# Splitting the weights once and reloading both parts from DRAM, in a hybrid decoder layer on one core

## The chip, the core and the metric

The kernel runs on one core of a Trainium2 chip. Times are microseconds (us) of device time, from one execution of the whole program. The median of three runs of the kernel before is 2899.07 us (2898.01 to 2899.21). A change of about 0.2%, 5.8 us, is the least that a measurement of this kernel can tell from no change.

The engines are called as the profile calls them: PE is the matrix engine and PEld its loading of weights, DVE the vector engine, ACT the scalar engine, POOL the general engine, and SP the engine that only issues transfers. Each works through its own instructions in a fixed order.

## What is computed

The reference is one decoder layer over 2048 tokens of width 1024, batch 1, all in 32-bit floats. Cut to what matters here:

```python
mod = (cs @ ada_w[l] + ada_b[l])[:, None, :]
sh1, sc1, g1, sh2, sc2, g2 = jnp.split(mod, 6, axis=-1)
h = rmsnorm(x, norm1_g[l]) * (1.0 + sc1) + sh1
p = h @ w_in[l]
...
y = jnp.concatenate([ya, yb, yc], axis=-1) * mix_beta[l]
x = x + g1 * (y @ w_out[l])
h = rmsnorm(x, norm2_g[l]) * (1.0 + sc2) + sh2
x = x + g2 * swiglu(h, ffn_w_gate[l], ffn_w_up[l], ffn_w_down[l])
```

ya, yb and yc come from three recurrent mixers (RG-LRU, HGRN2, RWKV-7) that read columns of p. Five weight matrices multiply activations of every token: w_in (1024 x 3456), w_out (1024 x 1024), w_gate and w_up (1024 x 2816 each) and w_down (2816 x 1024).

## The kernel before

**Tiling.** Activations lie transposed, 128 features by 512 tokens in a tile. The 2048 tokens make four blocks, b = 0 to 3. Weights lie in DRAM in chunks of 128 output columns: w_in has 27 of them (128 x 1024 each), w_out 8, w_gate and w_up 22 each, and w_down 8 chunks of 2816.

**Precise products from reduced floats.** A 32-bit product is made from three matmuls of the faster format (R in the code): every operand is split into a high part, which is the value rounded to that format, and a low part, which is the rest. `project` (line 238) adds high x high, high x low and low x high for each 128 rows of the contraction: three matmuls of 128x128 by 128x512 on line 248. The product of 512 contraction rows, one piece of weights, is twelve matmuls.

**Weights.** `load_w` (line 227) cuts the weights that it is given into pieces of 512 contraction rows. For each it loads the raw piece on SP's queue into a tile `wr` (`raw_w`, line 129; three buffers, 256 KB), and then splits it (`split_v`, line 219): ACT copies it to `wh` with rounding (recorded on line 78), and DVE subtracts to get `wl` (line 221). `wh` and `wl` have four buffers each. A buffer of `wr` comes free with its subtraction, one of `wh` and `wl` with the last matmul that reads it. The conditioning weights (`ada_w`, line 172 through line 140) use `wr` too after the start.

**How often.** A piece is loaded and split anew each time that a block needs it. The stage of w_in takes the blocks in pairs (0 and 1, then 2 and 3): of the 27 chunks, 18 serve both blocks of a pair from one load, and the first four and last five of the order are loaded once for each block. That makes 36 chunks in a pair, 72 in all, two pieces each. After it, for each block in turn, `w_out_products` (line 892) goes through the 8 chunks of w_out, and `ffn` (line 922) through 22 of w_gate and w_up (`ffn_up`, line 906) and through w_down in six groups of four (the last of two) feature tiles for each of eight output chunks, so that its last eight pieces have 256 rows only.

**Mixers.** The products of w_in go to DRAM (`pd`, stored on SP's queue, line 867). The mixers of a block load their columns on ACT's queue (line 461), run as long chains of small instructions on PE, DVE and ACT with round trips through DRAM (the tiles NL, NX and GIQ, lines 583 to 611), and store their results in `yd`. `load_y` (line 883) loads these for `w_out`; POOL does the subtraction there (line 217).

**What sets the order.** A planner orders each engine's instructions when the program is built, from its own estimates of times. An instruction is taken when its inputs and a buffer for its output are there in the plan, the lowest number first; the numbers come from the levels of line 62: "out" before "load" before "feed" before "mix" before "dense". Loads and splits of weights are "load", loads of x and stores of `pd` are "feed", the mixers are "mix", the matmuls of line 248 are "dense", and so are the stores of the output (line 943). On the chip each engine keeps the planned order whatever the true times are. `w_after` (lines 131 to 134) holds a load of weights behind another load at the start.

**Norms.** After w_out and before the next w_in there is a norm: squares are summed, `rstd_of` (line 288) splits the sum into tiles of `w_parts` (line 224) and sends it through PE with ones (lines 296 to 299), and `make_h` (line 322) makes the split activations `hh` and `hl` for the next products.

Of the kernel before, what the change touches and what calls it, by code (L numbers as in the profile page):

```python
# [10 lines left out]
F = mybir.dt.float32  # L11
R = mybir.dt.float32r
# [8 lines left out]
TB = 512  # L21
# [30 lines left out]
def hybrid_kernel(ctx, tc, x, par, ada_w, w_in, rgw, igw, w_up, a_up, g_up, w_out,  # L52
# [169 lines left out]
        return i  # L222

    def w_parts():
        return dp.tile([128, TB], R, name="wh", bufs=4), dp.tile([128, TB], R, name="wl", bufs=4)

    def load_w(src, fn):
        ws = []
        with level("load"):
            for c in range(0, src.shape[1], TB):  # L230
                n = min(TB, src.shape[1] - c)
                w = raw_w(src[:, c:c + n])
                hi, lo = w_parts()
                fn(w[:, :n], hi[:, :n], lo[:, :n])
                ws.append((hi, lo))
        return ws

    def project(h, *cols):
# [113 lines left out]
    with level("feed"):  # L352
        xsum = None
        xt = [load_x(x, 0, k) for k in range(KC)]
        w_after[:] = last_load
        tiles = {}
        for k in range(KC):
            for part, tile in ((1, tr_), (0, th_)):
                tiles[part, 0, k] = ada_tile(tile(), part, 0, k)
        for k in range(KC):  # L360
            for part, tag in ((1, "hh"), (0, "hl")):
                tiles[part, 1, k] = ada_tile(dp.tile([128, TB], F, name=tag, bufs=16), part, 1, k)
        for k in range(KC):
            xsum = square_sum(xsum, xt[k], k)
        rs = rstd_of(xsum)

        def shift_and_scale(half, pe):
            drain(zip_longest(*(ada(part, half, lambda k, part=part: tiles[part, half, k], pm_, xs_, pe)
                                for part in (1, 0))))

        shift_and_scale(0, (0, 2, 4))
        head = IN_ORDER[:2]
        W = {c: load_w(w_in[c], split_v) for c in head}
        w_after[:] = last_load
        h0 = make_h(lambda k: xt[k], rs, A1, B1, ks=range(4))
        ahead = x_stats([1], 8, tr_, th_, lambda: (tile_of("th", R)[:, 0:TB], tile_of("th", R)[:, 0:TB]))
        next(ahead)
        shift_and_scale(1, (0, 1))
        h0 += make_h(lambda k: xt[k], rs, A1, B1, ks=range(4, KC))
# [6 lines left out]
    with level("mix"):  # L386
# [14 lines left out]
        w = th_()  # L401
# [450 lines left out]
    def w_in_products(h, cols, side):  # L852

        n = 0
        while n < len(cols):

            cs_ = cols[n:n + 2] if n == 0 and len(h) == 1 else cols[n:n + 1]
            ws = [W.pop(c) if c in W else load_w(w_in[c], split_v) for c in cs_]
            for i, b in enumerate(h):
                for j, (c, p) in enumerate(zip(cs_, project(h[b], *ws))):  # L860
                    with level("feed"):
                        t = xs_()
                        if (n + i + j) % 2:
                            act(t, p)
                        else:
                            V.tensor_copy(t, p)
                        SP.dma_start(pd[c, :, b * TB:(b + 1) * TB], t)
                    next(side, None)
            n += len(cs_)
# [22 lines left out]
    def w_out_products(b, ys, before):  # L892
        x1, s = [], None
        for d in range(KC):
            ws = load_w(w_out[d], split_v)
            t = load_x(x, b, d)
            p, = project(ys, ws)
            with level("out"):
                stt(t, p, G1[:, d:d + 1], t, OP.mult, OP.add)
            if d == 0:  # L900
                before()
            s = square_sum(s, t, d)
            x1.append(t)
        return x1, rstd_of(s)

    def ffn_up(h, f):
        if f:
            p, = project(h, load_w(w_gate[f], split_v))
        else:
            p, pu = project(h, load_w(w_gate[f], split_v), load_w(w_upf[f], split_v))  # L910
        t = xs_()
        with level("out"):
            act(t, p, AF.Silu)
        if f:
            pu, = project(h, load_w(w_upf[f], split_v))
        with level("out"):
            V.tensor_mul(t, pu, t)  # L917
        g = parts_()
        split_v(t, *g)
        return g  # L920

    def ffn(b, x1, rs):
        h = make_h(lambda k: x1[k], rs, A2, B2, "silu_and_others", over=False)
        gs, s, ys = [], None, None
        for f0 in range(0, NF, 4):
            n = min(4, NF - f0)
            while len(gs) < min(f0 + n + (2 if f0 + n + 2 >= NF else 1), NF):
                gs.append(ffn_up(h, len(gs)))
            if len(gs) == NF and ys is None and b + 1 < NB:
                ys = load_y(b + 1)  # L930
            for d in range(KC):
                p, = project(gs[f0:f0 + n], load_w(w_down[d][:, f0 * 128:(f0 + n) * 128], split_v))
                with level("out"):
                    stt(x1[d], p, G2[:, d:d + 1], x1[d], OP.mult, OP.add)
                if f0 + n == NF:
                    s = square_sum(s, x1[d], d, n=1 if b + 1 < NB else 2)
# [96 lines left out]
```

## Time and profile before

| | before |
|---|---|
| median of 3 runs | 2899.07 us |
| profiled execution, its own time | 2902.32 us |
| span from first to last instruction in it | 2900.5 us |
| mean granted PE clock | 0.979 |
| HBM read, written | 286.53 MB, 48.23 MB |

The profiled execution is 3.25 us over the median, and 1.8 us of its time lie outside the span. The profile counts an engine as busy from the start of its first to the end of its last overlapping instruction; matmuls overlap, so their busy times don't add up. "Idle before" is the time that an engine stood still before an instruction, and the name behind the arrow is what ended the wait. A name with a small q is the engine's own queue, where transfers are issued. The granted clock is the share of its full speed at which PE was let run.

### The profile page before, as it was taken

The page shows a single profiled execution, that of the slowest core. Times are in us where ns is not written, and L with a number is a line of the kernel's source. Part 1 is how long each engine was busy: PE and PEld are TensorE (multiplying, and loading weights), DVE is VectorE, ACT ScalarE, POOL GpSimd, SP SyncE. Part 2 cuts the span into 40 slices and gives each one's busy share as a digit, 9 for nine tenths or more (in the row PEclk, how much of TensorE's full clock was granted, in tenths as well). Part 3 has the DMA queues.
Part 4 walks back from the last instruction along what each step waited for, and adds up shares of the span by engine and source line. Part 5 has one row for each costly group of instructions (what it writes and reads, how often), then busy time and mean ns, then how long its engine had stood idle before and what let it go on. Part 6 is the DMA issues. An engine that isn't in the chain of part 4 may idle for free. (4 is left out here: it accounts for less than half of the span.)

```text
span 2900.5 us, 41766 instructions
## 1 busy us (share of the span) xinstructions
PE 2771.4 (96%) x14842; PEld 2197.8 (76%) x14842; DVE 1985.5 (68%) x4617; ACT 1506.6 (52%) x2521; POOL 82.4 (3%) x67
## 2 busy tenths in 40 slices
PE   7999998999998899999999999999899999999998
PEld 6777776777776677777767777777677788788886
DVE  7765867777577687777887877778776444644345
ACT  4528456254645846567576465675563433533333
POOL 2000000000001000000100000010000001000000
PEclk9999999999999999999999999999999999999999
DMA  7534445434344233333442323335233233433332
GB/s 253 155 116 131 135 145 185 141 119 131 99 128 138 84 95 87 106 103 95 142 138 84 113 70 116 98 103 162 65 93 101 88 98 116 145 99 98 98 95 87
DMA packets 235041, 337.52 MB, mean 116 GB/s; under 512 B 73041, under 2 KB 78673, under 8 KB 234833
## 3 DMA queue, kind: packets, MB, share of 16 engines
q1 hardware_dynamic: 160144, 285.55, 31.7%
q10 hardware_dynamic: 74688, 49.31, 6.9%
q8 instruction: 117, 1.92, 0.3%
q14 instruction: 92, 0.75, 0.1%
HBM read 286.53 MB, written 48.23 MB: 115 GB/s over the span
## 5 line engine op out<-in xcount | busy, mean ns | idle before, releaser
L248 PE MATMUL pd<-hh,wh 128*128 128x512 f32 x3232 | 1290.5, 400 | 31.5 <-ACT hh L78 31.1
L248 PE MATMUL pd<-hl,wh 128*128 128x512 f32 x3232 | 1290.6, 399 | 4.9 <-DVE hl L81 2.7
L248 PE MATMUL pd<-hh,wl 128*128 128x512 f32 x3232 | 1290.8, 399 | 0.0
L78 ACT ACTIVATE wh<-wr 128x512 fp32r<-128x512 f32 (+1 forms) x752 | 462.1, 619 | 870.0 <-PE pd L248 666.5
L248 PEld LDWEIGHTS pd<-hh,wh 128*128 128x128 f32 x3232 | 613.9, 190 | 161.2 <-ACT hh L78 35.8
L221 DVE TENSOR_TENSOR wl<-wr,wh 128x512 fp32r<-128x512 f32 (+1 forms) x752 | 509.2, 682 | 309.8 <-ACT wh L78 304.4
L248 PEld LDWEIGHTS pd<-hl,wh 128*128 128x128 f32 x3232 | 613.9, 190 | 136.6 <-DVE hl L81 7.8
L248 PEld LDWEIGHTS pd<-hh,wl 128*128 128x128 f32 x3232 | 614.0, 190 | 123.4 <-issue 2.6
L81 DVE SCALAR_TENSOR_TENSOR xs<-pd,Q,xs 128x512 f32<-128x512 f32 x224 | 167.6, 748 | 127.3 <-PE pd L248 120.4
L78 ACT ACT_TABLE_LOAD x190 | 243.8, 1283 | 12.1 <-DMA GIQ<-xd 3.3
L78 ACT ACTIVATE xs<-pd 128x512 f32<-128x512 f32 x140 | 82.8, 591 | 59.7 <-PE pd L248 55.2
L917 DVE TENSOR_TENSOR xs<-pd,xs 128x512 f32<-128x512 f32 x88 | 60.7, 690 | 75.0 <-PE pd L248 73.8
L78 ACT ACTIVATE th<-th 128x512 f32<-128x512 f32 (+2 forms) x153 | 93.5, 612 | 31.1 <-DMA th<-pd 9.0
L78 ACT ACTIVATE hh<-xs 128x512 fp32r<-128x512 f32 x120 | 74.2, 627 | 41.2 <-DVE xs L917 31.3
L78 ACT ACTIVATE hw<-VS,we 64x64 f32<-64x64 f32 x192 | 66.0, 344 | 47.1 <-DVE VS L81 44.0
L599 DVE TENSOR_TENSOR ftmp<-NX,NL 128x30 f32<-128x30 f32 (+4 forms) x360 | 75.2, 209 | 8.8 <-DMA NX<-nd 1.3
L601 DVE TENSOR_TENSOR NX<-NX,ftmp 128x30 f32<-128x30 f32 (+4 forms) x360 | 74.8, 208 | 7.7
L529 POOL MEMSET KG<- 64x1024 f32 x24 | 22.7, 947 | 1775.4 <-PE pm L642 671.0
L78 ACT ACTIVATE xs<-xs 128x512 f32<-128x512 f32 x77 | 47.7, 627 | 41.4 <-DVE xs L81 26.8
L81 DVE SCALAR_TENSOR_TENSOR VS<-pc,we,hw 64x64 f32<-64x64 f32 x168 | 47.4, 282 | 31.7 <-PE pc L653 28.3
L78 ACT ACTIVATE tr<-tr 128x512 f32<-128x512 f32 (+3 forms) x100 | 62.4, 627 | 11.9 <-DVE tr L81 8.3
L221 DVE TENSOR_TENSOR hl<-xs,hh 128x512 fp32r<-128x512 f32 x88 | 61.8, 702 | 5.7 <-ACT hh L78 1.3
(234 smaller groups left out, 2697.6 us busy)
## 6 DMA issues: line engine op xcount, KB each, us to landing
wr<-in_w_gate SPq DMA_DIRECT2D x176, 256.0 KB, 2.6
wr<-in_w_upf SPq DMA_DIRECT2D x176, 256.0 KB, 2.6
wr<-in_w_down SPq DMA_DIRECT2D x160, 256.0 KB, 2.7
wr<-in_w_in SPq DMA_DIRECT2D x144, 256.0 KB, 3.4
pd<-xs SPq DMA_DIRECT2D x108, 256.0 KB, 3.1
xs<-in_x SPq DMA_DIRECT2D x72, 256.0 KB, 4.5
wr<-in_ada_w SPq DMA_DIRECT2D x64, 256.0 KB, 3.4
th<-pd ACTq DMA_DIRECT2D x64, 256.0 KB, 3.5
```

What stands on the lines that cost most here:

```text
L78: return A.activation(o, i, f, **k)
L81: return V.scalar_tensor_tensor(o, a, s, b, op0=op0, op1=op1)
L221: V.tensor_sub(lo, src, hi.bitcast(F))
L248: PE.matmul(p, a[:, c], b, start=(n == 0), stop=(n == tot - 1))
L529: G.memset(KG[o, :, :, e], 0.0)
L599: V.tensor_mul(tv, NX[:, 0:m, j:j + 1].to_broadcast([128, m, n]), NL[:, j:j + 1, j + 1:32].to_broadcast([128, m, n]))
L601: V.tensor_add(NX[:, 0:m, j + 1:32], NX[:, 0:m, j + 1:32], tv)
L917: V.tensor_mul(t, pu, t)
```

## The change

`load_w` gets a name and a number in place of the splitting function, from which a key is made for each piece. At the first use of a key the piece is loaded raw and split as before, into the two halves of one tile `wp` (four buffers, 512 KB each, in place of four of `wh` and four of `wl`), and `wp` is then stored in a new DRAM tile of that key on SP's queue. At any later use of the key both halves are loaded by one transfer on SP's queue straight into `wp`, with no instruction on ACT or DVE. `w_parts`, which the norms use, now takes the halves of a `wp` tile.

```diff
     def w_parts():
-        return dp.tile([128, TB], R, name="wh", bufs=4), dp.tile([128, TB], R, name="wl", bufs=4)
-
-    def load_w(src, fn):
+        t = dp.tile([128, 2, TB], R, name="wp", bufs=4)
+        return t[:, 0], t[:, 1]
+
+
+    parted = {}
+
+    def load_w(src, name, i, first=0):
+
         ws = []
         with level("load"):
             for c in range(0, src.shape[1], TB):
                 n = min(TB, src.shape[1] - c)
-                w = raw_w(src[:, c:c + n])
-                hi, lo = w_parts()
-                fn(w[:, :n], hi[:, :n], lo[:, :n])
-                ws.append((hi, lo))
+                t = dp.tile([128, 2, TB], R, name="wp", bufs=4)
+                key = f"{name}{i}_{first + c}"
+                if key in parted:
+                    k = SP.dma_start(t[:, :, :n].bitcast(F), parted[key])
+                    if w_after:
+                        order(k, w_after.pop())
+                else:
+                    w = raw_w(src[:, c:c + n])
+                    split_v(w[:, :n], t[:, 0, :n], t[:, 1, :n])
+                    parted[key] = tc.dram_tile([128, 2, n], F, name=key)
+                    SP.dma_start(parted[key], t[:, :, :n].bitcast(F))
+                ws.append((t[:, 0], t[:, 1]))
         return ws
...
-        W = {c: load_w(w_in[c], split_v) for c in head}
+        W = {c: load_w(w_in[c], "i", c) for c in head}
...
-            ws = [W.pop(c) if c in W else load_w(w_in[c], split_v) for c in cs_]
+            ws = [W.pop(c) if c in W else load_w(w_in[c], "i", c) for c in cs_]
...
-            ws = load_w(w_out[d], split_v)
+            ws = load_w(w_out[d], "o", d)
...
-            p, = project(h, load_w(w_gate[f], split_v))
+            p, = project(h, load_w(w_gate[f], "g", f))
...
-                p, = project(gs[f0:f0 + n], load_w(w_down[d][:, f0 * 128:(f0 + n) * 128], split_v))
+                p, = project(gs[f0:f0 + n], load_w(w_down[d][:, f0 * 128:(f0 + n) * 128], "d", d, f0 * 128))
```

The other calls in `ffn_up` change in the same way ("g" for w_gate, "u" for w_up).

More of the change, by code (lines that the diff above doesn't have):

```diff
@@ L907, in ffn_up @@
         if f:
-            p, = project(h, load_w(w_gate[f], split_v))
+            p, = project(h, load_w(w_gate[f], "g", f))
         else:
-            p, pu = project(h, load_w(w_gate[f], split_v), load_w(w_upf[f], split_v))
+            p, pu = project(h, load_w(w_gate[f], "g", f), load_w(w_upf[f], "u", f))
         t = xs_()
@@ L914, in ffn_up @@
         if f:
-            pu, = project(h, load_w(w_upf[f], split_v))
+            pu, = project(h, load_w(w_upf[f], "u", f))
         with level("out"):
```

## The prediction

> **What bounds the kernel now.** I read the busy line first, then the groups with shapes kept apart.
>
> ```profile
> PE 2771.4 (96%) x14842; PEld 2197.8 (76%) x14842; DVE 1985.5 (68%) x4617; ACT 1506.6 (52%) x2521; POOL 82.4 (3%) x67
> ```
> ```profile
> L248 PE MATMUL pd<-hh,wl 128*128 128x512 f32 x3232 | 1290.8, 399 | 0.0
> L248 PEld LDWEIGHTS pd<-hh,wh 128*128 128x128 f32 x3232 | 613.9, 190 | 161.2 <-ACT hh L78 35.8 <-issue 4.1 <-ACT wh L78 0.7
> L221 DVE TENSOR_TENSOR wl<-wr,wh 128x512 fp32r<-128x512 f32 x720 | 496.0, 694 | 309.8 <-ACT wh L78 304.4 <-PE pd L248 2.7
> L78 ACT ACTIVATE wh<-wr 128x512 fp32r<-128x512 f32 x720 | 448.9, 629 | 835.1 <-PE pd L248 632.9 <-issue 78.9 <-DMA wr<-in_w_in 50.5
> ```
>
> PE is busy all but 129.1 us of the span. It hardly waits for weights: 0.7 us for `wh`, nothing before a matmul with `wl`. It is the other way round: ACT's splits wait 633 us for PE to free a buffer. Next come PE's rate and idle time by stage (columns: stretch, length, busy us and instructions of PE, PEld, DVE, ACT, POOL; clock, DMA share, GB/s).
>
> ```profile
> 430.00:860.00 430.00, 408.48 (x2405) 322.61 (x2404) 311.14 (x779) 218.86 (x376) 3.79 (x4) 0.98 0.45 135
> 860.00:1440.00 580.00, 556.86 (x3156) 435.52 (x3156) 443.90 (x1090) 352.09 (x586) 28.49 (x22) 0.98 0.36 105
> 1440.00:1960.00 520.00, 500.96 (x2884) 396.01 (x2883) 400.75 (x971) 333.52 (x549) 18.28 (x14) 0.98 0.36 105
> 1960.00:2480.00 520.00, 506.48 (x2493) 402.90 (x2492) 328.29 (x720) 243.29 (x417) 13.32 (x10) 0.98 0.35 104
> 2540.00:2880.00 340.00, 340.00 (x1502) 281.63 (x1501) 141.63 (x213) 103.71 (x172) 0.00 (x0) 1.00 0.32 95
> ```
>
> The last row is the last block, with no mixers beside it: 1502 matmuls in 340 us, 0.226 us each, not one gap. All 9696 matmuls of line 248 at that price are 2195 us; the mixers' PE work fills most of the rest. So the change works on engines that don't bound. It can win only idle time, and the clock lost around it, in the stages that reuse weights: about 430 to 860 (second pair of w_in) and 1440 to 2480 (blocks 1 and 2). Their idle time is 21.5 + 19.0 + 13.5 = 54.0 us. Here are its largest pieces, with two of the last block for comparison.
>
> ```profile
> 493.64 0.79 PE L248 MATMUL pd<-hh,wh 128*128 128x512 f32 x1 [10.66 <-ACT hh L78]
> ```
> ```profile
> 617.88 0.65 PE L653 MATMUL pc<-VS,BK 128*128 128x128 f32 x2 [2.87 <-ACT VS L78]
> ```
> ```profile
> 1956.40 0.79 PE L257 MATMUL pm<-tr,bones 128*128 128x512 f32 x1 [5.76 <-ACT tr L78]
> ```
> ```profile
> 2040.38 0.49 PE L298 MATMUL pd<-wl,aones 128*128 128x512 f32 x1 [1.52 <-DVE wl L221]
> 2042.79 2.08 PE L299 MATMUL pd<-xs,ones 128*128 128x512 f32 x2 [1.91 <-DVE xs L281]
> 2049.12 1.22 PE L248 MATMUL pd<-hh,wh 128*128 128x512 f32 x2 [4.26 <-ACT hh L78]
> ```
> ```profile
> 2517.63 1.12 PE L299 MATMUL pd<-xs,ones 128*128 128x512 f32 x2 [1.57 <-DVE xs L281]
> 2523.02 1.22 PE L248 MATMUL pd<-hh,wh 128*128 128x512 f32 x2 [4.26 <-ACT hh L78]
> ```
>
> A norm costs PE 1.57 + 4.26 = 5.8 us even with nothing beside it. Three norms lie in the reusing stages, so of the 54.0 us at most 54.0 - 17.5 = 36.5 us can go.
>
> **What goes.** First uses are 54 pieces of w_in (27 chunks of two), 16 of w_out, 44 each of w_gate and w_up, 48 of w_down: 206 of 752 splits stay and 546 go, 24 of them of half size, counted here as halves. DVE loses (522 + 12) x 0.694 = 371 us, ACT (522 + 12) x 0.629 = 336 us. Neither is on PE's path as a sum. What counts is which splits stood ahead of a chain that PE waited for:
>
> ```profile
> 1942.53 1.12 DVE L221 TENSOR_TENSOR wl<-wr,wh 128x512 fp32r<-128x512 f32 x1
> ...
> 1947.64 1.10 DVE L221 TENSOR_TENSOR wl<-wr,wh 128x512 fp32r<-128x512 f32 x1
> ```
> ```profile
> 2040.24 1.89 DVE L221 TENSOR_TENSOR wl<-wr,wh 128x512 fp32r<-128x512 f32 x3
> 2042.05 0.69 DVE L281 TENSOR_TENSOR xs<-xs 128x512 f32<-128x512 f32 x1
> ```
>
> - Before the wait of 5.76 us DVE ran without a pause, these two splits among its work: 2.2 us.
> - Three splits stand directly ahead of the sum (line 281) that PE awaits at 2042.79: 1.9 us.
> - The 10.66 us at 493.64 are a norm whose eight loads of x were issued behind a load of weights that waited for a split (SP's timeline below). Its floor is 5.8; I take back the excess, 4.8 us (bounds 0 and 4.8).
> - At 617.88 ACT was late; I take 1.4 of 2.87.
> - The rest is 54.0 - 10.66 - 2.87 - 5.76 - 7.69 = 27 us of smaller waits. DVE loses 371/1985 = 19% of its work; I take 19%, 5 us (bounds 0 and 27 - 5.8 = 21, less the norm of block 1).
>
> ```profile
> 486.50 0.33 SPq L131 DMA_DIRECT2D wr<-in_w_in  x1
> 486.88 4.58 SPq L140 DMA_DIRECT2D xs<-in_x  x8
> ```
>
> Sum 15 us. What also goes is ACT's holding: the 633 us for which it stood before a split until PE freed `wh`, with the mixers' and norms' work behind it in its order. I count that within these waits, because it reaches the time only through them. The clock adds a little:
>
> ```profile
> 480.00:500.00 20.00, 8.73 (x30) 6.26 (x29) 18.57 (x32) 8.22 (x12) 0.00 (x0) 0.66 0.75 246
> 600.00:620.00 20.00, 17.13 (x91) 14.05 (x90) 11.13 (x29) 10.39 (x24) 0.00 (x0) 0.95 0.49 155
> ```
>
> Around a long wait PE runs slow: 0.34 x 20 = 6.8 us of clock are gone in the first of these, and 1 us after the wait of 2.87 in the second. Part of that falls into the wait itself; for waits shortened but mostly not removed I take 3 us (bounds 0 and 10). **Gain: 18 us.** The Trainium skill ("TensorE: Matmul & The Clock Gate", Part 1) has the clock fall only after an idle window of about 3.4 us. By that, shortening the small waits would return no clock; the 0.95 beside a wait of 2.87 us speaks against it as a sharp limit, and the sum would differ by 1 to 3 us.
>
> **What is added.** *Loads twice as long, waiting for PE.* A reload waits on SP for a buffer of `wp`, that is for PE's last matmul on the piece four back, where the raw loads ran up to seven pieces ahead. Behind it on SP stand loads of x and y, for which `make_h`, the residual sums and the splits of y wait on DVE and ACT; stores of `pd` and `out`, whose tiles `xs` the next products' copies out of PE's banks need; and the conditioning loads, for DVE. The plan never puts a load there before its buffer is free in the plan, so the wait costs where the chip falls behind the plan.
>
> ```profile
> wr<-in_w_down SPq DMA_DIRECT2D x160, 256.0 KB, 2.7
> ...
> wr<-in_w_down SPq DMA_DIRECT2D x32, 128.0 KB, 2.0
> ```
>
> 128 KB more cost 0.7 us, so 512 KB should land in 2.7 + 1.4 = 4.1 us (an estimate from these rows). Three pieces lie between: 3 x 12 x 0.226 = 8.1 us of PE's work, more where mixers run or a piece serves two blocks. About 4 us stay spare. In w_down's last eight pieces there are 3 x 6 x 0.226 = 4.1 us against 2.7 and the issue: 1 us spare. I take +3 us for three such ends (bounds 0, and 3 x 8 x 1.36 = 33 if every load there were late by a piece). Traffic in blocks 1 to 3 rises by 176 x 256 KB = 46 MB in some 520 us, from 105 to about 194 GB/s.
>
> *Stores at first use.* 206 stores wait on DVE's split, as the raw load three pieces on already does, so SP loses only their issue:
>
> ```profile
> L867 SPq DMA_DIRECT2D pd<-xs x108: 319/327/424, 61.3 to 879.3; - x108
> ```
>
> A store of `pd` takes 0.327 us to issue, so 206 x 0.327 = 67 us over two stages in which SP mostly waits: nothing. A buffer of `wp` is free only when its store has landed too; four pieces of PE's work lie before its next use, and I count nothing. In block 0 they add 144 x 512 KB over 580 us, 130 GB/s, to 105; the profile has shown
>
> ```profile
> 20.00:40.00 20.00, 18.90 (x84) 17.98 (x83) 14.86 (x27) 5.83 (x8) 0.00 (x0) 1.00 1.03 370
> ```
>
> 370 GB/s, so I put block 0 at nothing; raw loads there still run ahead. But this very window is full, and the first four pieces are stored about there: 2.1 MB at 370 GB/s is 5.7 us on the conditioning loads that the first products need. I take +3 (bounds 0 and 5.7). The norm's use of `wp` in place of `wh` and `wl` takes the same one of four: nothing.
>
> **Sum**: -18 + 3 + 3 = -12 us on the profiled execution: 2902.3 to 2890.3. The median of the runs stood 3.25 us lower: **2887 us**, 0.4% faster.
>
> **Rivals.**
>
> *Nothing moves* (2893 to 2905). The floors stay, freed time on DVE and ACT is filled by mixers that the planner brings forward, and PE meets other waits of the same size. For it: the pure dense row has no gap to win, and the end waits for PE. That reuse fails to happen belongs here too; the keys look distinct, so hardly.
>
> *All contention goes* (2858). 36.5 us of idle and 10 of clock, less the 6 added: 2899 - 41. For it: ACT's long holds on PE vanish from the mixers' path.
>
> *SP becomes the bound* (2928). With PE's own progress at SP's head, a store waiting there holds back the next piece:
>
> ```profile
> SPq L867 <- ACT xs L78: 128.7, 37, 7.8
> SPq L867 <- DVE xs L866: 121.7, 43, 8.5
> ...
> SPq L943 <- DVE xs L81: 29.3, 18, 15.0
> ```
>
> (total, times, longest.) Today seven pieces hide this. It decides from a wait over the 4 us spare: the three longest exceed it by 3.8 + 4.5 + 11 = 19 us, and three new idle stretches lose about 3 us of clock each: +28 with nothing won elsewhere, and the next such waits would add as much again. Against: the mean wait is 1.6 to 3.5 us, and much of it is only SP being early today.
>
> *The mixers' small transfers slow down* (2912). They share the DMA engines with loads of twice the size.
>
> ```profile
> wr<-in_w_gate SPq DMA_DIRECT2D x176, 256.0 KB, 2.6
> ...
> wr<-in_w_in SPq DMA_DIRECT2D x144, 256.0 KB, 3.4
> ```
>
> In the stage of w_in, at 135 GB/s, a load takes 0.8 us more than in the blocks at 105. At 194 I put as much again on four round trips in each of 12 units of RWKV: 38 us, of which a third, as a guess, reaches PE: +13 with nothing won.
>
> ```profile
> 2265.77 209.03 PE pd L248 x922
> ```
>
> Against: the mixers end with 209 us of pure products left in block 2. The Trainium skill ("DMA: Bandwidth & Descriptors", Queues, rings and completion order) says that an engine switches between queues only after a whole packet of several descriptors, which speaks for this rival; no row here shows the switching itself.
>
> **How the numbers follow.** Forecast 0.44 (own range 2866 to 2893), all contention goes 0.11, nothing moves 0.20, SP 0.16, transfers 0.09. Faster by over 0.2% (about what a measurement of this kernel can tell) 0.55, within 0.20, slower 0.25. The range 2857 to 2935 leaves out the tail of the large gain and the part of the SP case where more such waits follow.
>
> **What would show it.** DVE busy near 1614 us, ACT near 1171, 206 splits. Right: PE's idle in 430 to 860 and 1440 to 2480 falls from 54 to about 38 us, the wait for `hh` at the second pair near 6, and matmuls of line 248 hardly wait for `wp` loads. Wrong: PE waits on DMAs of weights, or SP's stores with reloads late behind them; landings far over 4.1 us; more than 0.226 us per matmul in the last block.

## The result, and the profile after

| | before | after |
|---|---|---|
| median | 2899.14 us (2898.01 to 2904.67, 4 runs) | 2976.62 us (2968.55 to 2976.93, 4 runs) |
| ratio, with its 95% interval | | 1.0257 (1.0235 to 1.0278) |
| profiled execution, its own time | 2902.32 us | 2968.55 us |
| its span | 2900.5 us | 2966.8 us |
| mean granted PE clock | 0.979 | 0.969 |

The changed kernel is 2.6% slower, some 75 us, where 0.4% faster was forecast. The busy line of the profile after:

```profile
PE 2797.8 (94%) x14842; PEld 2212.9 (75%) x14842; DVE 1646.5 (55%) x4071; ACT 1163.0 (39%) x1952; POOL 79.9 (3%) x67
```

The relief of the two engines came as forecast, and the time still went up: DVE lost 339 us of work and ACT 344, PE has the same 14842 instructions, and the span of the profiled execution grew by 66.3 us. PE's idle time went from 2900.5 - 2771.4 = 129.1 us to 2966.8 - 2797.8 = 169.0. The clock took from 0.021 x 2900.5 = 61 us to 0.031 x 2966.8 = 92 us. Idle time and clock cost 40 and 31 us more than before, which is the whole loss with a little to spare.

By stages (stretch, length, busy us and instructions of PE, PEld, DVE, ACT and POOL, clock, DMA share, GB/s), first two stretches of the kernel before that the prediction doesn't show, then the changed kernel:

```profile
0.00:100.00 100.00, 80.08 (x324) 65.80 (x325) 80.56 (x163) 57.39 (x91) 14.73 (x13) 0.97 0.70 231
100.00:430.00 330.00, 315.85 (x1842) 245.44 (x1840) 226.29 (x608) 161.47 (x283) 3.79 (x4) 0.98 0.44 131
```
```profile
0.00:100.00 100.00, 66.51 (x262) 54.58 (x263) 69.88 (x143) 46.99 (x71) 14.15 (x13) 0.93 0.75 260
100.00:480.00 380.00, 356.07 (x2016) 279.79 (x2015) 254.68 (x657) 198.49 (x332) 4.24 (x4) 0.97 0.65 212
480.00:950.00 470.00, 441.11 (x2741) 342.15 (x2739) 309.38 (x883) 207.25 (x369) 5.69 (x6) 0.96 0.54 165
950.00:1580.00 630.00, 591.16 (x3225) 456.61 (x3226) 461.35 (x1120) 348.76 (x590) 29.86 (x22) 0.95 0.68 224
1580.00:2120.00 540.00, 521.15 (x3020) 406.96 (x3018) 343.31 (x968) 243.10 (x414) 15.80 (x14) 0.98 0.54 169
2120.00:2540.00 420.00, 413.71 (x1814) 339.20 (x1814) 104.32 (x155) 64.27 (x101) 10.16 (x8) 0.99 0.62 201
2600.00:2900.00 300.00, 300.00 (x1325) 248.43 (x1324) 51.70 (x72) 24.62 (x40) 0.00 (x0) 1.00 0.59 194
```

Length minus PE's busy time is its idle time. In the stages in order (start, first pair of w_in, second pair, block 0, block 1, block 2) it was 19.9, 14.2, 21.5, 23.1, 19.0 and 13.5 us before, and is 33.5, 23.9, 28.9, 38.8, 18.9 and 6.3 us after. PE stands idle 13.6 us longer at the start, 9.7 and 7.4 in w_in and 15.7 in block 0, as long as before in block 1, and 7 us less in block 2. The bounds of the stages are set by eye, so a few us may lie on either side of one. The three stages with the largest losses are the ones that store; the second pair of w_in, which only reloads, loses 7.4. The last block is as before: 1325 matmuls in 300 us, 0.226 us each.

What the memory had to move, before and after:

```profile
DMA packets 235041, 337.52 MB, mean 116 GB/s; under 512 B 73041, under 2 KB 78673, under 8 KB 234833
```
```profile
DMA packets 268788, 583.34 MB, mean 197 GB/s; under 512 B 76336, under 2 KB 87088, under 8 KB 268592
```

246 MB more: some 106 MB of stores and 140 MB of reloads that are twice as long as the raw loads. The weights come in time, as a row further down shows; what comes late are other transfers. The time from issue to landing of both kinds (line, queue, count, size of one, median us), before and then after:

```profile
tr<-pd ACTq DMA_DIRECT2D x44, 256.0 KB, 3.5
NX<-nd ACTq DMA_DIRECT2D x48, 32.0 KB, 2.3
GIQ<-xd ACTq DMA_DIRECT2D x48, 32.0 KB, 2.6
```
```profile
wp<-g SPq DMA_DIRECT2D x132, 512.0 KB, 3.3
wp<-i SPq DMA_DIRECT2D x90, 512.0 KB, 4.0
wp<-o SPq DMA_DIRECT2D x48, 512.0 KB, 4.7
tr<-pd ACTq DMA_DIRECT2D x44, 256.0 KB, 4.4
NX<-nd ACTq DMA_DIRECT2D x48, 32.0 KB, 3.9
GIQ<-xd ACTq DMA_DIRECT2D x48, 32.0 KB, 3.2
```

The same mixers' transfers land 0.6 to 1.6 us later. DVE waited longer for transfers. The three rows that grew most (total us, times, longest), before and then after:

```profile
DVE pcar L468 <- DMA tr<-pd: 10.3, 9, 2.2
DVE xs L81 <- DMA xs<-in_x: 5.1, 7, 1.4
DVE tr L617 <- DMA GIQ<-xd: 3.0, 3, 2.5
```
```profile
DVE pcar L481 <- DMA tr<-pd: 29.0, 15, 5.7
DVE tr L630 <- DMA GIQ<-xd: 25.0, 10, 5.1
DVE xs L81 <- DMA xs<-in_x: 22.9, 11, 3.8
```

18.4 us of such waits have become 76.9. PE itself waits for a weight transfer almost never:

```profile
PE pd L261 <- DMA wp<-i: 3.5, 3, 1.2
```

With the pieces of w_down and w_out, 1.0 and 0.3 us in the same view, that is 4.8 us in all.

Not all of DVE's 58 us more reach PE. So three causes were to be told apart: the bytes, which slow the others' transfers; the place of the stores in SP's order; and the order of all engines' instructions, which the planner makes anew for a changed program.

### The profile page after: what moved, and what is told of

The parts are those of the page before. It is cut to its first block, busy times and chain, and to the rows that moved or that the text cites. A ratio compares the mean times of both kernels' runs of the same rounds, so it can differ in the third digit from the quotient of the medians.

```text
span 2966.8 us, 40236 instructions
## 1 busy us (share of the span) xinstructions
PE 2797.8 (94%) x14842; PEld 2212.9 (75%) x14842; DVE 1646.5 (55%) x4071; ACT 1163.0 (39%) x1952; POOL 79.9 (3%) x67
## 2 busy tenths in 40 slices
DMA packets 268788, 583.34 MB, mean 197 GB/s; under 512 B 76336, under 2 KB 87088, under 8 KB 268592
## 4 chain that ended last, share of the span: by engine, by line
PE 66%; DVE 13%; DMA 11%; ACT 7%; issue 3%; SPq 1%; ACTq 0%; DVEq 0%; POOL 0%; POOLq 0%
PE pd L261 53%; DVE xs L81 2%; PE pm L583 1%; ACT L78 1%; DMA tr<-pd 1%; DMA wr<-in_ada_w 1%; DMA th<-pd 1%; ACT tr L78 1%; DVE wp L221 1%; DVE ftmp L612 1%; DVE NX L614 1%; ACT th L78 1%; ACT wp L78 1%; DMA xs<-in_x 1%; PE ph L790 1%
## 5 line engine op out<-in xcount | busy, mean ns | idle before, releaser
L261 PE MATMUL pd<-hh,wp 128*128 128x512 f32 x6464 | 2104.5, 401 | 38.7 <-ACT hh L78 25.0
L261 PEld LDWEIGHTS pd<-hh,wp 128*128 128x128 f32 x6464 | 1222.5, 191 | 294.7 <-ACT hh L78 28.9
L261 PE MATMUL pd<-hl,wp 128*128 128x512 f32 x3232 | 1300.9, 402 | 4.1 <-DVE hl L81 2.7
L261 PEld LDWEIGHTS pd<-hl,wp 128*128 128x128 f32 x3232 | 617.3, 191 | 135.0 <-DVE hl L81 7.5
L78 ACT ACTIVATE wp<-wr 128x512 fp32r<-128x512 f32 (+1 forms) x206 | 126.4, 619 | 177.6 <-PE pd L261 86.9
L221 DVE TENSOR_TENSOR wp<-wr,wp 128x512 fp32r<-128x512 f32 (+1 forms) x206 | 141.7, 696 | 69.0 <-ACT wp L78 67.2
L78 ACT ACTIVATE th<-th 128x512 f32<-128x512 f32 (+2 forms) x153 | 93.8, 614 | 66.3 <-DVE th L800 20.6
L612 DVE TENSOR_TENSOR ftmp<-NX,NL 128x30 f32<-128x30 f32 (+4 forms) x360 | 76.0, 211 | 16.8 <-DMA NX<-nd 5.5
L221 DVE TENSOR_TENSOR hl<-xs,hh 128x512 fp32r<-128x512 f32 x88 | 60.7, 690 | 35.2 <-ACT hh L78 34.9
L78 ACT ACTIVATE VS<-pc 64x64 f32<-64x64 f32 x96 | 21.1, 219 | 97.5 <-DVE VS L664 95.3
```

What stands on the lines that cost most here:

```text
L78: return A.activation(o, i, f, **k)
L221: V.tensor_sub(lo, src, hi.bitcast(F))
L261: PE.matmul(p, a[:, c], b, start=(n == 0), stop=(n == tot - 1))
L612: V.tensor_mul(tv, NX[:, 0:m, j:j + 1].to_broadcast([128, m, n]), NL[:, j:j + 1, j + 1:32].to_broadcast([128, m, n]))
```

## The experiments

All sixteen kernels were timed beside the kernel before on the same chip. Its median moved between 2893.75 and 2901.21 us from chip to chip, so the ratio is what counts; "us" below is (ratio - 1) x 2899. Diffs are against the changed kernel unless another is named, and show the lines that matter only. e4, e5 and e6 leave out each piece's own parts: every reload reads one and the same piece.

| kernel | ratio (95%) | us | MB moved |
|---|---|---|---|
| changed kernel | 1.0257 (1.0235 to 1.0278) | +74.5 | 583.34 |
| e1 one tile for both parts, nothing else | 0.9904 (0.9877 to 0.9932) | -27.8 | 337.52 |
| e8 the same, two chunks of w_in swapped | 0.9922 (0.9893 to 0.9951) | -22.6 | as e1 |
| e12 kernel before, the same swap | 1.0010 (0.9990 to 1.0029) | +2.9 | as before |
| e11 changed kernel, the same swap | 1.0219 (1.0178 to 1.0260) | +63.5 | as after |
| e5 reloads of half size, no stores | 0.9942 (0.9920 to 0.9965) | -16.8 | 337.93 |
| e4 reloads of full size, no stores | 1.0050 (1.0030 to 1.0070) | +14.5 | 477.92 |
| e6 e4 with six buffers | 1.0130 (1.0106 to 1.0154) | +37.7 | 477.92 |
| e9 e1 with raw loads of double size | 1.0087 (1.0061 to 1.0114) | +25.2 | 477.51 |
| e2 stores, no reuse | 1.0182 (1.0151 to 1.0213) | +52.8 | 443.46 |
| e3 e2 with stores of 8 columns | 1.0073 (1.0045 to 1.0101) | +21.2 | 339.24 |
| e10 e3 on POOL's queue | 0.9950 (0.9925 to 0.9975) | -14.5 | 339.25 |
| e13 e2 with stores of one row | 1.0061 (1.0043 to 1.0079) | +17.7 | 338.37 |
| e14 e13 on POOL's queue | 0.9931 (0.9916 to 0.9946) | -20.0 | 338.39 |
| e7 changed kernel, stores on POOL's queue | 1.0306 (1.0269 to 1.0344) | +88.7 | 583.35 |
| e15 changed kernel, first four pieces not kept | 1.0137 (1.0113 to 1.0161) | +39.7 | 578.10 |
| e16 e15 with stores on POOL's queue | 1.0198 (1.0173 to 1.0223) | +57.4 | 578.11 |

### The merged tile alone, and whether it is luck of the order

The change does more than it says: two tiles of four buffers become one of four. e1 has only this.

```diff
-                if key in parted:
-                    k = SP.dma_start(t[:, :, :n].bitcast(F), parted[key])
...
-                else:
-                    w = raw_w(src[:, c:c + n])
-                    split_v(w[:, :n], t[:, 0, :n], t[:, 1, :n])
-                    parted[key] = tc.dram_tile([128, 2, n], F, name=key)
-                    SP.dma_start(parted[key], t[:, :, :n].bitcast(F))
+                w = raw_w(src[:, c:c + n])
+                split_v(w[:, :n], t[:, 0, :n], t[:, 1, :n])
```

> Every piece is split at every use as before, into one tile of two halves; no store and no reload: the merged tile and a newly made plan alone. If the stores or the reloads are what costs, 2890 to 2910 us (before 2899). If the merged tile ties PE to the subtraction, or a new plan alone can cost as much, 2940 us or more.

It takes 2873.5 us (2869.38 to 2878.74), ratio 0.9904, below either forecast: **faster than both kernels**, and by more than the whole change was forecast to bring. The planner orders anew when a tile changes, so the gain could have been one lucky order. e8, e11 and e12 swap two neighbours of the order of w_in's chunks, in e1, in the changed kernel and in the kernel before:

```diff
-IN_ORDER = (25, 26, 19, 16, 22, 7, 4, 10, 13, 0, 2, 20, 17, 23, 8, 5, 11, 14, 1, 3, 21, 18, 24, 9, 6, 12, 15)
+IN_ORDER = (25, 26, 19, 16, 22, 7, 4, 10, 13, 0, 2, 17, 20, 23, 8, 5, 11, 14, 1, 3, 21, 18, 24, 9, 6, 12, 15)
```

> The kernel with the merged tile alone (2873.5), with two neighbouring w_in chunks swapped in the order: the same work under another plan. If plans of the same work differ little, 2865 to 2882 us. If a plan's luck is worth tens of us, anywhere between 2850 and 2910 us, and differences of that size between the other kernels carry no cause.

> The changed kernel with two neighbouring w_in chunks swapped in the order: the same work under another plan. If a plan's luck is small, 2965 to 2985 us; if it is worth tens of us, outside of that.

> The kernel before with the same swap. If the merged tile is what gains 28 us, 2890 to 2908 us. If the kernel before merely had an unlucky plan, 2870 to 2885 us.

The merged tile keeps its gain (-28 and -23 us), and the kernel before doesn't move with the swap (+3, its interval holds 1). But the traces show that the swap was no test of the order in these two. Compared by operation and tile names, all 14842 of PE's matmuls stand at the same place in e8 as in e1, and in e12 as in the kernel before: another chunk is loaded, and nothing is ordered anew. Between the kernel before and e1 only 8855 of them do. So e8 is a second measurement of e1, 5 us away, and whether the 28 us come from the tile or from the order that came with it stays open. In the changed kernel the swap did make another order (7814 places the same). Its ratio is 11 us lower; the changed kernel's ratio lies just inside e11's wide interval, and the median lies under the 2965 to 2985 us forecast for a small effect of the order. As much as that of a difference between two kernels with different orders may be order alone.

### Reuse without its bytes, and bytes without reuse

e4 reuses as the change does, but stores one piece only and reloads that one every time, so that the stores are gone. e5 is e4 with a reload of one half, which both factors of the products read, so that a reload moves as much as a raw load did.

```diff
-                    k = SP.dma_start(t[:, :, :n].bitcast(F), parted[key])
+                    k = SP.dma_start(t[:, :, :n].bitcast(F), parted["one"][:, :, :n])     # e4
+                    k = SP.dma_start(t[:, 0, :n].bitcast(F), parted["one"][:, 0, :n])     # e5
...
```

> Reuse as in the change, 512 KB for each later use, but only the very first piece is stored and every reload reads that one, so the products are computed with the wrong weights. No other stores. If the stores cost, faster than before: 2870 to 2895 us, PE idle in blocks 1 and 2 under 30 us. If the reloads cost, 2930 to 2965 us with losses in the second pair of w_in and in blocks 1 to 3.

> As the kernel with reloads only, but each reload takes 256 KB into one half, and both halves' matmuls read that half (wrong weights): the same waits of SP for PE, half the bytes. If the bytes of the reloads cost (slower round trips of the mixers), 2865 to 2885 us against 2914 of the full reload. If SP's tie to PE costs, 2905 to 2925 us.

e4 gives 1.0050, between the two forecasts. It is the plainest answer to where the loss comes from: without the stores the change costs 14.5 us in place of 74.5. e5 gives 0.9942, so that e4, with 140 MB more, is 31 us slower than e5. And e5, from which 546 splits are gone with no byte added, is no faster than e1, which makes them all: 11 us slower by the ratios, though their intervals overlap, and 6 us slower than e8. So the work taken from DVE and ACT won nothing that can be measured. All these pairs differ in their order too.

e9 turns it round: every use is split as in e1, nothing is stored or reloaded, and only the raw load of each later use fetches twice what is needed.

```diff
-                w = raw_w(src[:, c:c + n])
+                if key in parted:
...
+                    w = raw_w(src[:, c:c + n], a[:, s:s + 2 * n], o - s)
+                else:
+                    w = raw_w(src[:, c:c + n])
+                    parted[key] = True
```

> The kernel with the merged tile alone (2873.5), splits at every use, with the raw load of each later use taking twice its bytes (512 KB, of which the split reads half): 140 MB more, no reload, no store, ACT and DVE as busy as ever. If bytes cost by slowing the mixers' and norms' transfers, as 34 us between the full and the half reload suggest, 2895 to 2915 us. If the full reload lost by its own lateness before PE, 2870 to 2882 us, since raw loads run ahead.

For this the three buffers of `wr` are doubled. e9 gives 1.0087, 53 us over e1 by the two ratios and 2 us above the range forecast for the bytes. The traffic of e9 (e1 moves 337.52 MB in as many packets), and what DVE waited for in e1 and then in e9:

```profile
DMA packets 235040, 477.51 MB, mean 164 GB/s; under 512 B 73040, under 2 KB 75600, under 8 KB 234832
```
```profile
DVE xs L81 <- DMA xs<-in_x: 8.9, 10, 2.6
DVE tr L623 <- DMA GIQ<-xd: 3.6, 4, 2.0
```
```profile
DVE xs L81 <- DMA xs<-in_x: 21.0, 11, 6.1
DVE tr L634 <- DMA GIQ<-xd: 10.8, 6, 3.9
```

The number of packets is the same, so only their length has changed. The work is that of e1, and the loads of x and the mixers' round trips come late, at a mean of 164 GB/s where 370 had been seen in the start of the kernel before. Two things keep the 53 us from being the price of the others' delay alone: the order is another one (7140 of PE's matmuls at the same place), and the longer raw loads of w_in are themselves late for ACT's splits, which waited 60.7 us for them in e9 and 29.9 in e1.

### More lead for the reloads

If the lead of four buffers were too short, six would help. e6 is e4 with six, here and in `w_parts`:

```diff
-                t = dp.tile([128, 2, TB], R, name="wp", bufs=4)
+                t = dp.tile([128, 2, TB], R, name="wp", bufs=6)
```

> As the kernel with reloads only, with six buffers of wp in place of four: the lead of a reload over PE grows from three pieces to five, the bytes stay. If the short lead and SP's tie to PE cost, 2865 to 2890 us. If the bytes cost, 2900 to 2920 us.

It is 23 us slower than e4 by the ratios, above both forecasts. So nothing speaks for a short lead of the reloads as what costs. Why this kernel is slower was not followed up; its order is another one too.

### The stores: place or bytes

e2 splits at every use and stores at the first, as the change does. e3 stores only 8 columns of each half, in the same place on SP; e10 puts e3's stores on POOL's queue.

```diff
-                if key in parted:
...
-                else:
-                    w = raw_w(src[:, c:c + n])
-                    split_v(w[:, :n], t[:, 0, :n], t[:, 1, :n])
+                w = raw_w(src[:, c:c + n])
+                split_v(w[:, :n], t[:, 0, :n], t[:, 1, :n])
+                if key not in parted:
...
+                    SP.dma_start(parted[key], t[:, :, :n].bitcast(F))    # e2
+                    SP.dma_start(parted[key], t[:, :, :8].bitcast(F))    # e3
+                    G.dma_start(parted[key], t[:, :, :8].bitcast(F))     # e10
```

> Split at every use as before, and the parts stored at the first use; nothing is reloaded. Theory that the stores cost (their place on SP, their bytes, their hold on the tile): about 2899 + 17 at the start + 25 in the w_in stage + 30 to 45 in block 0 = 2960 to 2985 us, slower than the changed kernel if the reuse itself wins in block 2. Theory that the reloads cost (shorter lead, PE at the head of SP): 2900 to 2920 us.

> As the kernel with stores only, but each store takes 8 columns of each half (8 KB in place of 512 KB): SP waits for the same splits, the bytes are gone. If the bytes cost, 2895 to 2910 us; if the wait of SP's store for the split costs, within 15 us of the kernel with full stores.

> The kernel with stores of 8 columns (2923.6), with these stores on POOL's queue. If a store's place on SP, waiting for DVE with other transfers behind it, costs the 50 us over the merged tile, 2870 to 2890 us. If they come from the store's hold on wp or from the plan, 2910 to 2935 us.

e2 comes out just under its first range, and is not slower than the changed kernel. Stores of 8 columns, 1.7 MB in all, still take e3 49 us above e1, between its two forecasts; the full bytes add 32 (e2). On POOL's queue the same small stores cost 13. But e3 has 56,034 packets more than e1 and e10 only 6,595, so place and packets were not yet apart. e13 and e14 store one row of 4 KB instead (the diff is against e3):

```diff
-                    SP.dma_start(parted[key], t[:, :, :8].bitcast(F))
+                    SP.dma_start(parted[key], t[:1, :, :n].bitcast(F))   # e13
+                    G.dma_start(parted[key], t[:1, :, :n].bitcast(F))    # e14
```

> Every use is split, as in the kernel with stores of 8 columns, but the store at first use takes one row of wp (4 KB) on SP's queue instead of 128 rows of 8 columns: the store's place at SP's head stays, 56,000 small packets go. If the place cost the 36 us between that kernel on SP's and on POOL's queue, this one lands near it, 1.006 to 1.009 of the kernel before. If the small packets cost it, this one lands near the merged tile alone and near the 8 columns on POOL, 0.990 to 0.996.

> The same one-row store on POOL's queue. With the place as the cost: 0.990 to 0.996, some 30 us under the one-row store on SP. With the packets as the cost: level with the one-row store on SP, within 8 us.

e13, with 430 packets more than e1, is as slow as e3, so the packets aren't it. e14 is 38 us faster by the ratios, 38.9 by the medians (2916.75 and 2877.81). **Small stores on SP cost some 38 us more than on POOL, counting the order that the planner makes with them**: e14 keeps e1's order, and e13 has another (6913 of PE's matmuls at the same place).

e2 and e13 differ in the bytes of the stores alone: PE's order is the same at all 14842 places. **The bytes of the stores, 105 MB, cost 35 us** (1.0182 and 1.0061). In block 0, from 950 to 1580 us, PE's idle time is 23.6 us in e13 and 37.5 in e2, and over the whole kernel DVE waits 5.5 us for the mixers' loads of `NX` in e13 and 11.2 in e2.

The trace shows what the place does. SP's own timeline at the start, e13 and then e14 (start, us, queue, line, transfer, count):

```profile
15.44 1.42 SPq L243 DMA_DIRECT2D i<-wp  x3
...
18.73 0.43 SPq L140 DMA_DIRECT2D th<-in_ada_w  x1
24.36 0.24 SPq L243 DMA_DIRECT2D i<-wp  x1
24.64 0.33 SPq L140 DMA_DIRECT2D tr<-in_ada_w  x1
...
56.17 0.43 SPq L140 DMA_DIRECT2D tr<-in_x  x1
...
69.42 1.43 SPq L407 DMA_DIRECT2D th<-in_msk  x3
```
```profile
18.57 0.43 SPq L140 DMA_DIRECT2D tr<-in_ada_w  x1
...
50.01 0.42 SPq L140 DMA_DIRECT2D tr<-in_x  x1
...
52.93 2.75 SPq L407 DMA_DIRECT2D th<-in_msk  x3
```

In e13 SP stands from 19.2 to 24.4 before the fourth store, which waits for its split; behind it stand the conditioning loads, which need nothing. All that follows is some 5 us late, and the last load of x goes at 56.17 instead of 50.01. The masks of a mixer (`in_msk`) go at 69.42 instead of 52.93: in e14 they stand ahead of the first store of `pd`, in e13 behind two. PE's conditioning product and the next norm, e13 and then e14:

```profile
32.11 3.57 PE L184 MATMUL pm<-ones,xs 128*128 128x1 f32 x16 [5.08 <-DVE xs L81]
...
69.36 0.50 PE L306 MATMUL pd<-th,aones 128*128 128x512 f32 x1 [3.56 <-ACT th L78]
76.06 0.79 PE L307 MATMUL pd<-th,aones 128*128 128x512 f32 x1 [6.21 <-DVE th L221]
```
```profile
27.70 3.57 PE L184 MATMUL pm<-ones,xs 128*128 128x1 f32 x16 [0.66 <-DVE xs L81]
...
60.34 0.40 PE L306 MATMUL pd<-th,aones 128*128 128x512 f32 x1
61.85 0.39 PE L307 MATMUL pd<-th,aones 128*128 128x512 f32 x1
```

The conditioning product waits 4.4 us longer: that is the store at SP's head. The norm has two waits, 9.8 us in all, that e14 doesn't have, and these come from the order of SP, ACT and DVE. In e13 DVE makes the norm's second split at 75.32 only, after it stood 5.22 us for a mixer's load of `pd` and 1.84 us for the masks, which it has to take first there; in e14 it makes it at 60.85. The changed kernel shows both: the conditioning product waits 1.50 and 4.76 us where the kernel before waits 0.66, and the norm 3.64 and 4.07 us where the kernel before waits 0.32. These are 13.0 of the 13.6 us of idle time that it has more in the first 100 us. The first 100 us, e13 and then e14:

```profile
0.00:100.00 100.00, 66.65 (x258) 54.76 (x259) 70.58 (x144) 46.48 (x72) 13.72 (x13) 0.91 0.58 198
```
```profile
0.00:100.00 100.00, 79.84 (x332) 65.78 (x333) 80.01 (x163) 59.58 (x92) 20.08 (x23) 0.98 0.69 233
```

PE is busy 13.2 us less. It is busy 66.65 us with 4 KB stores on SP, 64.31 with stores of 512 KB in the same order (e2), and 79.84 with the stores elsewhere. So of the loss at the start the place and the order make 13 us, and the bytes that the prediction had looked at 2.3.

### Whole stores on POOL's queue

If the place costs 38 us, moving the changed kernel's stores should win them. e7 and e16 move them; e15 and e16 don't keep the first four pieces (each line below belongs to the kernels named beside it).

```diff
-                    SP.dma_start(parted[key], t[:, :, :n].bitcast(F))
+                    G.dma_start(parted[key], t[:, :, :n].bitcast(F))              # e7
+                    if name != "i" or i not in IN_ORDER[:2]:                      # e15, e16
+                        SP.dma_start(parted[key], t[:, :, :n].bitcast(F))         # e15
+                        G.dma_start(parted[key], t[:, :, :n].bitcast(F))          # e16
```

> The changed kernel with its 206 stores issued on POOL's queue in place of SP's, the bytes unchanged. If the stores' place on SP costs most (head of line), 2915 to 2940 us against 2977, with no loss at the start beyond 6 us. If their bytes cost most, 2955 to 2980 us.

> The changed kernel, but the first two chunks of w_in (four pieces) are never stored and are split at each of their four uses; the other pieces are stored on SP's queue and reloaded. Tells what the stores cost that meet the conditioning loads at the start. If PE's 16 to 18 us lost in the first 100 us come from these four stores, this kernel is 12 to 18 us faster than the changed one: 1.019 to 1.022. If the loss there comes from elsewhere, 1.025 as the changed one.

> The same with the stores on POOL's queue. The changed kernel with its stores on POOL lost 15 us of PE at the start, which is gone here. If a store at SP's head costs 36 us, this kernel is well under the same with stores on SP: 25 to 36 us faster, 0.99 below in ratio. If the place costs little and the bytes and packets do, the two are level within 8 us.

e7 is 14 us *slower* than the changed kernel, with intervals that overlap, and above both forecasts. It says more beside e4: but for the stores the two are one kernel, with PE's order the same at 14835 of 14842 places, and e7 is 74 us slower. **105 MB more of stores cost 74 us, though no store stands on SP's queue.** PE's idle time grows by 14 us in the first pair of w_in (100 to 480 us) and by 18 in block 0 (950 to 1580), the stages that store.

e16, on POOL, is 18 us slower than e15, on SP. Neither came out as expected. The first 100 us of e15, then of e16:

```profile
0.00:100.00 100.00, 69.90 (x275) 57.67 (x276) 72.29 (x149) 48.90 (x76) 13.67 (x13) 0.91 0.69 231
```
```profile
0.00:100.00 100.00, 80.04 (x331) 65.72 (x332) 78.98 (x160) 57.72 (x89) 17.75 (x19) 0.98 0.80 274
```

The start is repaired in e16 alone. In e15 the conditioning product waits 0.66 us again, so the four stores were what held it; but the norm's two waits are still 3.79 and 7.09 us, because the order with stores on SP puts them there. e16 gives its gain back and more in w_in and in blocks 0 and 1. A store of w_in takes longer there (e15, then e16):

```profile
i<-wp SPq DMA_DIRECT2D x50, 512.0 KB, 3.4
```
```profile
i<-wp POOLq DMA_DIRECT2D x50, 512.0 KB, 5.4
```

Whether that or the other order makes e16 slower stays open. So the 38 us of the place, measured with small stores, could not be won back with whole ones. e15 also beat the changed kernel by 35 us where 12 to 18 were expected. Of that only 3.4 us of PE's time lie in the first 100 us; the rest comes later, in another order (7222 of PE's matmuls at the same place). So not keeping four pieces of 206 moves the time by about as much as a whole cause. The changed kernel may have an unlucky order, by some 11 us (e11) to 30 us (e15); no run shows which part of the order it is.

### What the terms make together

How far two kernels can be compared depends on their order. The table gives for each pair how many of PE's 14842 matmuls stand at the same place.

| from | to | what differs | same place | us |
|---|---|---|---|---|
| e13 | e2 | bytes of the stores, on SP | 14842 | +35 |
| e4 | e7 | whole stores on POOL's queue | 14835 | +74 |
| e1 | e14 | stores of 4 KB on POOL's queue | 14842 | +8 |
| e1 | e10 | stores of 8 KB on POOL's queue | 14842 | +13 |
| e4 | changed | whole stores on SP | 7122 | +60 |
| e14 | e13 | small stores from POOL to SP | 6913 | +38 |
| e5 | e4 | bytes of the reloads | 9004 | +31 |
| e1 | e9 | bytes of raw loads | 7140 | +53 |
| e1 | e5 | reuse without bytes | 6008 | +11 |
| before | e1 | merged tile | 8855 | -28 |

In the first four rows the order is the same, so what differs is the cause. In the others the number is that of the change and of the order that came with it. Merged tile, reuse, bytes of the reloads, bytes of the stores, place and the rest of small stores add up to -28 + 11 + 31 + 35 + 38 + 8 = +95, and +74.5 was measured. The terms don't simply add: e15 has all of them but four pieces, and is at +40, only 22 us over e13. What is shown is that the stores make most of the loss (+60 with another order, +74 on POOL with the same), and that their bytes cost by themselves. More bytes are slower in each pair made for it (e5 to e4, e1 to e9, e13 to e2), and small stores on SP are slower than on POOL twice (e10 to e3, e14 to e13). How the rest divides between place and order isn't shown.

## Why the prediction was wrong

**The bound and the counts: right.** DVE was forecast near 1614 us and has 1646.5, ACT near 1171 and has 1163.0, and the splits are 206. PE bounds, the last block runs at 0.226 us per matmul before and after, and only idle time and clock could change.

**The gain, 18 us: wrong in its size, with a part right.** The wait for `hh` at the second pair was forecast near 6:

```profile
521.48 1.22 PE L261 MATMUL pd<-hh,wp 128*128 128x512 f32 x2 [4.90 <-ACT hh L78]
```

It fell from 10.66 to 4.90. But idle time in the reusing stages, forecast to fall from 54.0 to about 38, is 28.89 + 18.85 + 6.29 = 54.0. In the second pair idle time grew by 7.4 us though its longest wait had shrunk by 5.8, and in block 2 it fell by 7.2. And in e5, without added bytes, no gain shows either: it is 11 us behind e1, 6 behind e8. "I take 19%, 5 us" for the small waits assumed that PE waits on DVE in proportion to DVE's work; no run bears that out.

**The reloads' lead, +3 us: right.** PE waited 4.8 us for weight transfers in all. 4.1 us to land was the estimate, 3.3 to 4.7 is what they took. More buffers didn't help (e6). The 176 pieces in the working are a slip: a block reloads 152, eight of them of half size, which makes 39 MB and an estimate of 180 GB/s in place of 194; 169 and 201 were measured in the stretches of blocks 1 and 2. The rival "SP becomes the bound" as it was put, with stores and reloads late against PE, was not what happened to the reloads; but its place, a store waiting at SP's head, was the right one in the storing stages.

**The stores, put at "nothing" and +3 us at the start: the step that failed.** Without them the change costs 14.5 us (e4), with them 74.5. The next three paragraphs take the three places where the working dealt with them.

**"SP loses only their issue ... nothing": failed.** It compared the store's wait for the split with the raw load three pieces on, which waits for the same split. It left out what stands between the two in SP's order, the conditioning loads first, and that the planner would order the other engines around the stores. The two together cost 38 us with small stores (e14 to e13), of which 13 lie in the first 100 us; the wait at SP's head alone is seen in the 4.4 us of the conditioning product. The working had itself asked for the queue behind a waiting instruction at the reloads, and not at the stores. The changed kernel's own queue shows the waits (total us, times, longest):

```profile
SPq L247 <- DVE wp L221: 377.5, 137, 15.4
```

Their sum is no price: SP's raw loads stood 1417.1 us for the same split in the kernel before. What counts is what stands behind.

**"So I put block 0 at nothing": failed.** A peak of 370 GB/s in a full window at the start says that bytes can be moved, not that others are not delayed. The stores' bytes cost 35 us in an unchanged order (e13 to e2), with 13.9 us more idle time of PE in block 0; in the changed kernel that idle time grew by 15.7.

**The start, +3 us (0 to 5.7): right for the bytes, too small for the start.** 13.6 us more idle time came. The bytes take 2.3 us (e13 to e2), the place and the order the rest, as e13 shows with 4 KB stores.

**The rival "the mixers' small transfers slow down": right in kind, mis-sized.** +13 was forecast. It was put on the reloading stages alone and on four round trips; the bytes also delay loads of x and `pd`, and they come with the stores too. Measured: +31 (e5 to e4) to +53 (e1 to e9) for 140 MB in loads, with another order in both, and +35 for the stores'. For the guess that a third reaches PE the working had no row. The rule of the Trainium skill cited there ("DMA: Bandwidth & Descriptors", Queues, rings and completion order) has the trace on its side in direction: 32 KB on ACT's queue land in 3.9 us instead of 2.3 while SP's queue moves more. The switching itself no run shows.

**The merged tile, "nothing": wrong.** With it and the order that came with it the kernel is 28 us faster (e1), in the change's favour. How much of that the changed kernel keeps isn't shown.

**The chances.** The two slower rivals took one cost each. What came is several at once: the stores' bytes, their place with its order, the reloads' bytes; the range's upper end, 2935, held the price of one. Two of the three had been set at "nothing" without a bound. That the planner makes another order had a word in "nothing moves" but no price; e11 puts it at some 11 us.

## What to carry to other kernels

Before moving work from an engine that doesn't bound to the memory, price the bytes at what they do to the small transfers that others wait for: here 105 MB of stores, at a mean of 150 GB/s, cost 35 us with every matmul in the same order. A transfer that waits on a queue holds everything planned behind it, so read the queue's order and name each thing that stands behind. Where a planner orders the program, compare the order of two kernels in their traces before their difference is given to a cause: a swap of chunks that was meant as another order had left it as it was. And try the by-products of a change by themselves: the kernel with the merged tile alone, a few lines of the diff, is 1% faster than the kernel before.

## What had not been expected of the hardware

**After a wait PE ran at half the clock for a long time.** PE's timeline in block 0 of the changed kernel, and the granted clock around it:

```profile
1063.43 0.61 PE L261 MATMUL pd<-hh,wp 128*128 128x512 f32 x2
1068.13 0.24 PE L634 MATMUL pm<-tr,GIQ 32*32 32x32 f32 x2 [4.08 <-DVE tr L630]
```
```profile
1070.00:1080.00 10.00, 10.00 (x69) 6.63 (x68) 2.53 (x12) 1.52 (x4) 0.00 (x0) 0.50 0.23 80
1080.00:1090.00 10.00, 10.00 (x62) 8.46 (x61) 4.44 (x16) 2.82 (x8) 0.00 (x0) 0.70 0.25 79
```

DVE's transpose, and so PE, waited for `GIQ<-xd`, four transfers of 32 KB that took 3.0 to 5.1 us to land here, where 2.6 was the median before. PE then had work without a gap, and the clock stood at 0.50 for ten microseconds and at 0.70 over the next ten: the wait of 4.08 us took 8 us of clock with it, by an estimate from these two rows. The Trainium skill ("TensorE: Matmul & The Clock Gate", Part 1) has the full clock back after some 3.4 us of sustained activity. Here, with 32x32 matmuls between the large ones, it took longer, some 17 us, from 1069 to 1086; that they are the cause wasn't tried. In the kernel before, after the wait of 2.87 us at 617.88, the clock was 0.54 up to 620 and 0.63 up to 622, and full from there on. So a small transfer that was late cost PE some 12 us here, three times its wait.

**A queue of POOL's is not a free place.** Stores of 4 KB and 8 KB from there cost 8 and 13 us in an unchanged order (e1 to e14 and e10). Whole ones of w_in took 5.4 us to land where SP's took 3.4 (e16, e15), and on top of the reloads they cost 74 us (e4 to e7); how much of that is the queue and how much the bytes isn't shown.
